# Another order of the query rows in attention: second half first, the last head from long rows to short, q and k turned one by one

## The chip, the core and the metric

The kernel runs on one core of a Trainium2 chip. The metric is the device time of one execution in microseconds (us). Five engines work side by side, each through its own queue in order: TensorE (PE in the profile, with its weight loads as PEld), VectorE (DVE), ScalarE (ACT), GpSimd (POOL) and SyncE (SP), which in this kernel issues nearly all DMA transfers. Semaphores between the queues make an instruction wait for what it needs. Matmul results go to PSUM; tiles in SBUF and PSUM come from pools with a fixed number of buffers, so that a new tile waits until the last reader of the old one in its place is done.

## The reference

One layer of a decoder on 1024 tokens of width 1024: normalise, one wide projection to q, k, v, u and g, then two branches: differential attention with 8 heads, and a convolution of width 31 per channel. Both are projected, gated and merged, and a SwiGLU follows. Attention, cut to what matters here:

```python
def probs(qb, kf):
    s = jnp.einsum('bhqd,bhkd->bhqk', qb, kf) * scale + bias
    s = jnp.where(causal, s, -jnp.inf)
    return jax.nn.softmax(s, axis=-1)

p = probs(qb1, k1f) - lamf * probs(qb2, k2f)
return jnp.einsum('bhqk,bhkd->bhqd', p, vf)
...
a = rms_norm(a, subln_w[l]) * (1.0 - lam_init)
y_a = a.reshape(B, S, ATTN_WIDTH) @ w_proj_attn[l]
```

Query block i (128 queries) sees the first (i+1) x 128 keys. Each query has two rows of scores (q1 with k1, q2 with k2).

## The kernel before

A float32 product is made from three matmuls on a high and a low part (lines 160, 161 and 162), so parts `hT_hi` and `hT_lo` of the normalised input lie in SBUF, and weights are split into `whi` and `wlo` on ScalarE and VectorE. The heads of attention are short on TensorE work, so projections that are needed later run among them as *fill*: `later` lists for each head which. An item `G` makes a slice of the gates (2 groups of 24 matmuls 128x512 each, stored in `g_d`), an item `Q` the q and k of a later head (`q_item`, 4 groups of 48 matmuls 128x256). The taps of the convolution (line 561, `acc`) fill VectorE in the same way (`bg.step`), by an estimate of each step's slack (`slack_of`).

Attention is a list of 64 steps, (head h, query block i), before in the natural order. A step does:

- `scores(h, i)`: for each of the two q/k pairs the scores in tiles of up to 512 keys (`SPLITS`), two matmuls for each (lines 1014 and 1015) into `sc`, a PSUM tile from a pool of three. VectorE adds the bias `tb`, keeps the minimum and puts the row into `E` (line 1016), ScalarE takes exp with the row sum (1021), VectorE combines both rows into `E` (1027 to 1030).
- `more(k)`: the next groups of fill. They must stand behind the scores of three steps before, and a scheduler may move them among the scores.
- `turn` of the step before: transposes of `E` (`pT`, line 1050), split by ScalarE and VectorE into `ph` and `pl`.
- `slot`: for a pair of query blocks b whose `turn` is done, `weigh` (`pW`, the product with v), two steps later `back` (`pB`, 1070), then at the head's end `subln` and `subln_T` (`pS`, 1091), which stores the head into `a_d` (SP, 1094). It also takes whatever stands in `late`.

`late` holds `turn_qk`, which transposes the q and k of half a head (`pQ`, 771), scales (778), makes the low part (780), and moves halves between partitions by DMAs on SP (781 to 792): six for q, three for k. A half is 512 queries or keys. The first half's entry is free at once, the second half's from its own head's first step. `load_bias` (tb, one buffer) goes out at a head's first step, `load_v` (vh and vl, one buffer each) after the last `weigh` of the head before.

After the 64 steps come the last `turn`, `weigh`, `back` and `subln`, and what is left of the fill: four groups, of G14 and G15. Behind that the projection of attention starts. It needs all heads: those of 0 to 3 are loaded back from `a_d` by DMAs on SP into tiles `early` (1210), split into `aTh` and `aTl` (line 120 and 125), and the first matmul of the projection reads `aTh` of head 0. The convolution's result is loaded on the same queue into `cT_lo` (1228), which takes the place of `hT_lo` in SBUF.

A scheduler sets the order of instructions on each engine from the program's order and its own estimates of time; an `after(...)` holds an instruction behind another.

Of the kernel before, what the change touches and what calls it, by code (L numbers as in the profile page):

```python
# [31 lines left out]
NT = S // P  # L32
# [25 lines left out]
def kernel(  # L58
# [28 lines left out]
    dve, act, pool, pe = nc.vector, nc.scalar, nc.gpsimd, nc.tensor  # L87
# [24 lines left out]
    def nm(s):  # L112
        uid[0] += 1
        return f"{s}_{uid[0]}"

    def f32(ap):
        return ap.bitcast(F32)

    def split_hi(dst, src):
        act.copy(dst, src)  # L120

    last_lo, last_mm = [None], [None]
# [4 lines left out]
    def after(ins):  # L127

        return nullcontext() if ins is None else tc.issue_after(ins)
# [35 lines left out]
    ident = cst.tile([P, P], F32, name="ident")  # L165
# [15 lines left out]
    one = ap.tile([1, P], F32, name="one", bufs=1)  # L181
# [58 lines left out]
    def pcol(key, k=0):  # L240
        c = col[key] + k
        return pvec[:, c : c + 1]
# [82 lines left out]
    class Stream:  # L325
# [12 lines left out]
        def next(self):  # L338
            self.fetch()
            return self.have.pop(0)  # L340
# [16 lines left out]
    def gemm_N(o, halves, shi, slo, i):  # L357
# [25 lines left out]
        ["Q1", "G0", "G1"],  # L383
        ["Q2", "G2"],
        ["Q3", "G3"],
        ["G4", "Q4", "G5"],
        ["G6", "Q5"],
        ["Q6", "G7"],
        ["G8", "G9", "Q7"],
        ["G10", "G11", "G12", "G13"],  # L390
        ["G14", "G15"],
    ]
# [344 lines left out]
    qkp = None  # L737
    T = {}
    late = []

    def q_item(h):
        halves = [ws.next(), ws.next()]
        t = {}
        T[h] = t
        for b in range(2):
            raw = qkp.tile([P, 4, 256], F32, tag="qkraw", name=nm("qkraw"), bufs=2)
            ss = sm.tile([P, 16], F32, tag="ss16", name=nm("ss16"))
            for i2 in range(2):
                o = pg()
                for e in range(2):  # L750
                    gemm_N(o[:, 256 * e : 256 * (e + 1)], halves, hT_hi, hT_lo, 4 * b + 2 * i2 + e)
                act.copy(raw[:, 2 * i2 : 2 * i2 + 2, :], o[:].rearrange("p (e c) -> p e c", c=256))
                jk = sm.tile([P, VD], F32, tag="jk", name=nm("jk"), bufs=1)[:, :HD]
                for g in range(8):
                    act.activation(  # L755
                        jk, o[:, g * HD : (g + 1) * HD], AF.Square, accum_out=ss[:, 8 * i2 + g : 8 * i2 + g + 1]
                    )
                if i2 == 0:
                    yield
            r = rstd_of(ss[:], 16, 1.0 / HD, fast=h > 0)  # L760
            r4 = raw[:].rearrange("p i (g d) -> p (i g) d", d=HD)
            dve.tensor_tensor(r4, r4, r.unsqueeze(2).to_broadcast([P, 16, HD]), op=ALU.mult)

            def turn_qk(b=b, raw=raw):


                dma = nc.sync.dma_start
                for z, key in enumerate(("q", "k")):
                    pt = pm("pQ")
                    for i in range(4):  # L770
                        pe.transpose(pt[:, i * P : (i + 1) * P], raw[:, i, z * P : (z + 1) * P], ident[:])
                    w = pcol(key + "n")

                    def part(j):
                        return qkp.tile([P, 512], F32R, tag=f"{key}s{j}", name=f"{key}s{j}_{h}_{b}", bufs=2 if key == "q" else 3)

                    s1, s2 = part(1), part(2)
                    act.activation(s1[:], pt[:], AF.Identity, scale=w)
                    lo = part(3) if key == "q" else qkp.tile([P, 512], F32R, tag="klo", name=f"klo_{h}_{b}", bufs=1)
                    dve.scalar_tensor_tensor(lo[:], pt[:], w, f32(s1[:]), op0=ALU.mult, op1=ALU.subtract)  # L780
                    dma(f32(s2[HD:, :]), f32(s1[HD:, :]))
                    if key == "q":
                        lo2 = part(4)
                        for one, two in ((s1, s2), (lo, lo2)):
                            if one is lo:
                                dma(f32(two[HD:, :]), f32(one[HD:, :]))
                            dma(f32(two[:HD, :]), f32(one[HD:, :]))
                            dma(f32(one[HD:, :]), f32(one[:HD, :]))
                        t["q", b] = (s1, lo), (s2, lo2)
                    else:  # L790
                        dma(f32(s2[:HD, :]), f32(lo[HD:, :]))
                        dma(f32(s1[HD:, :]), f32(lo[:HD, :]))
                        t["k", b] = s1, s2

            late.append((NT * h if b and h else 0, turn_qk))
            yield

    inatt = [False]
# [154 lines left out]
    n = 0  # L953
# [42 lines left out]
    def scores(h, i):  # L996
# [34 lines left out]
        dve.reciprocal(RL[h][:, i : i + 1], l[:, 0:1])  # L1031
        ES[h, i] = E[0]

    def turn(h, i):

        b = i // 2
        if (h, b) not in PT:
            ph = aps.tile([P, NT, 256], F32R, tag="ph", name=nm("ph"), bufs=1)
            pl = aps.tile([P, NT, 256], F32R, tag="pl", name=nm("pl"), bufs=1)
            pool.memset(f32(ph[:, 2 * b + 1, 0:P]), 0.0)  # L1040
            pool.memset(f32(pl[:, 2 * b + 1, 0:P]), 0.0)
            PT[h, b] = ph, pl
        ph, pl = PT[h, b]
        e = ES.pop((h, i))
        qs = slice((i % 2) * P, (i % 2 + 1) * P)
        for k0 in range(0, i + 1, 4):
            n = min(4, i + 1 - k0)
            pt = pm("pT")
            for k in range(n):
                pe.transpose(pt[:, k * P : (k + 1) * P], e[:, (k0 + k) * P : (k0 + k + 1) * P], ident[:])  # L1050
# [49 lines left out]

    inatt[0] = True
    load_v(0)
    steps = [(h, i) for h in range(H) for i in range(NT)]
    scm, weighs, backs, sublns = [], [], [], []
    fill = run(it for l_ in later for it in l_)
    plan = [sum(4 if it[0] == "Q" else 2 for it in l_) for l_ in later]
# [8 lines left out]
    last_fill = [None]  # L1115
# [6 lines left out]
    def slot(n, nq):  # L1122

        with after(last_fill[0]):
            for h, b, ar in ready(backs, n):
                back(h, b, ar)
                if b == NT // 2 - 1:
                    subln(h)
                    sublns.append((n + 1, h))
            for _ in range(nq):  # L1130
                if late[0][0] <= n:
                    late.pop(0)[1]()
            for h in ready(sublns, n):
                subln_T(h)
            for h, b in ready(weighs, n):
                backs.append((n + 2, (h, b, weigh(h, b))))
                if b == NT // 2 - 1 and h + 1 < H:
                    load_v(h + 1)

    def slack_of(h, i):  # L1140

        p = (i + 1) * plan[h] // NT - i * plan[h] // NT
        nk = (i + 1) * P
        t_pe = nk * (2.52e-3 + (2.5e-3 if i % 2 else 0.0)) + 5.15 * p
        t_dve = 0.4 + 4.2e-3 * nk + p + 0.3
        return max(0.0, t_pe - t_dve)

    slack = [slack_of(h, i) for h, i in steps]
    slack[-2:] = [0.0, 0.0]
    share = len(bg.todo) / sum(slack)  # L1150

    due = 0.0
    for n, (h, i) in enumerate(steps):
        if i == 0:
            load_bias(h)
        p = (i + 1) * plan[h] // NT - i * plan[h] // NT
# [109 lines left out]
    part = bp.tile([P, P], F32, tag="part", name="part", bufs=1)  # L1266
# [50 lines left out]
    for c in range(NE, NKT):  # L1317
        w = ws.next()
# [76 lines left out]
    for z, (c, ls) in enumerate(WO):  # L1395
# [15 lines left out]
        for t_ in ts_:  # L1411
            h = xa[t_][:, TOK[c]]
# [306 lines left out]
```

## Time and profile before

| | |
|---|---|
| median of 3 runs | 1768.08 us (1764.07 to 1768.32) |
| the profiled execution | 1767.17 us |
| its span | 1765.1 us |
| PE busy | 1749.3 us, 99% |
| DVE busy | 1272.9 us, 72% |
| ACT busy | 803.8 us, 46% |
| POOL busy | 28.8 us, 2% |
| attention with its fill | about 310 to 850 us of the span |

Span and busy times are those of the profiled execution, which is 2.07 us longer than its span. An engine's idle time counts only where it delays the end. PEclk in the page's slices is the granted clock of TensorE in tenths; where it falls to half, matmuls take twice the time.

### The profile page before, as it was taken

The page shows a single profiled execution, that of the slowest core. Times are in us where ns is not written, and L with a number is a line of the kernel's source. Part 1 is how long each engine was busy: PE and PEld are TensorE (multiplying, and loading weights), DVE is VectorE, ACT ScalarE, POOL GpSimd, SP SyncE. Part 2 cuts the span into 40 slices and gives each one's busy share as a digit, 9 for nine tenths or more (in the row PEclk, how much of TensorE's full clock was granted, in tenths as well). Part 3 has the DMA queues.
Part 4 walks back from the last instruction along what each step waited for, and adds up shares of the span by engine and source line. Part 5 has one row for each costly group of instructions (what it writes and reads, how often), then busy time and mean ns, then how long its engine had stood idle before and what let it go on. Part 6 is the DMA issues. An engine that isn't in the chain of part 4 may idle for free.

```text
span 1765.1 us, 25860 instructions
## 1 busy us (share of the span) xinstructions
PE 1749.3 (99%) x9377; PEld 1505.8 (85%) x9377; DVE 1272.9 (72%) x2173; ACT 803.8 (46%) x1885; POOL 28.8 (2%) x107
## 2 busy tenths in 40 slices
PE   9999999999999999999999999999999999999999
PEld 7898998988999998988888888888888888888887
DVE  7388878998989888986687534877667666665544
ACT  5111331657767776755557313643333333333332
POOL 2001000000000000000000000000000000000000
PEclk9999999999999999999999999999999999999999
DMA  6236363225444344352983544234544544697663
GB/s 207 95 115 215 108 181 105 89 80 159 107 123 130 88 114 135 89 166 72 327 275 108 167 167 143 90 102 147 176 149 158 177 154 138 202 360 249 214 215 131
DMA packets 255731, 274.81 MB, mean 156 GB/s; under 512 B 16066, under 2 KB 177898, under 8 KB 255604
## 3 DMA queue, kind: packets, MB, share of 16 engines
q1 hardware_dynamic: 253424, 266.40, 47.9%
q0 software_dynamic: 1744, 5.19, 1.1%
q8 instruction: 74, 1.21, 0.3%
q10 hardware_dynamic: 436, 1.58, 0.3%
q14 instruction: 53, 0.43, 0.1%
HBM read 176.07 MB, written 78.68 MB: 144 GB/s over the span
## 4 chain that ended last, share of the span: by engine, by line
PE 92%; DVE 2%; DMA 2%; ACT 2%; issue 0%; SPq 0%; ACTq 0%; DVEq 0%
PE acc L1573 22%; PE pg L160 14%; PE pg L161 14%; PE pg L162 14%; PE acc L487 12%; PE sc L1015 2%; PE sc L1014 2%; PE wo L160 2%; PE wo L162 2%; PE wo L161 2%; PE pT L1050 1%; DMA qs<-qs 1%; PE pg L840 1%; PE pW L160 1%; PE pW L162 1%; PE pW L161 1%
## 5 line engine op out<-in xcount | busy, mean ns | idle before, releaser
L561 DVE SCALAR_TENSOR_TENSOR acc<-u,cw,acc 128x1024 f32<-128x1024 f32 x240 | 306.9, 1279 | 2.7
L120 ACT CAST whi<-wraw 128x1024 fp32r<-128x1024 f32 x107 | 112.5, 1052 | 215.0 <-PE pg L161 121.7
L160 PE MATMUL pg<-hT_hi,whi 128*128 128x512 f32 x512 | 200.9, 392 | 0.8 <-ACT sgg L599 0.8
L161 PE MATMUL pg<-wlo,hT_hi 128*128 128x256 f32 x704 | 200.8, 285 | 0.0
L162 PE MATMUL pg<-hT_hi,wlo 128*128 128x512 f32 x512 | 200.8, 392 | 0.0
L161 PE MATMUL pg<-hT_lo,whi 128*128 128x512 f32 x512 | 200.6, 392 | 0.0
L160 PE MATMUL pg<-whi,hT_hi 128*128 128x256 f32 x704 | 199.9, 284 | 0.5 <-ACT jk L755 0.5
L162 PE MATMUL pg<-whi,hT_lo 128*128 128x256 f32 x704 | 200.4, 285 | 0.0
L125 DVE TENSOR_TENSOR wlo<-wraw,whi 128x1024 fp32r<-128x1024 f32 x107 | 130.5, 1219 | 67.7 <-ACT whi L120 67.4
L125 DVE TENSOR_TENSOR wlo<-draw,whi 128x1024 fp32r<-128x1024 f32 x75 | 91.8, 1224 | 89.4 <-ACT whi L120 85.6
L120 ACT CAST whi<-draw 128x1024 fp32r<-128x1024 f32 x75 | 79.1, 1055 | 129.6 <-PE acc L487 121.1
L160 PEld LDWEIGHTS pg<-whi,hT_hi 128*128 128x128 f32 x704 | 134.7, 191 | 2.3 <-ACT jk L755 0.9
L161 PEld LDWEIGHTS pg<-wlo,hT_hi 128*128 128x128 f32 x704 | 134.5, 191 | 1.3
L162 PEld LDWEIGHTS pg<-whi,hT_lo 128*128 128x128 f32 x704 | 134.7, 191 | 0.8
L487 PE MATMUL acc<-whi,wlo 128*128 128x512 f32 x308 | 119.9, 389 | 0.0
L487 PE MATMUL acc<-wlo,whi 128*128 128x512 f32 x308 | 119.8, 389 | 0.0
L160 PEld LDWEIGHTS pg<-hT_hi,whi 128*128 128x128 f32 x512 | 96.2, 188 | 20.6 <-ACT sgg L599 1.1
L1021 ACT ACTIVATE E<-E,mn 128x256 f32<-128x256 f32 (+7 forms) x128 | 99.5, 779 | 30.6 <-DVE mn L1016 28.6
L161 PEld LDWEIGHTS pg<-hT_lo,whi 128*128 128x128 f32 x512 | 96.2, 188 | 19.5 <-issue 0.6
L162 PEld LDWEIGHTS pg<-hT_hi,wlo 128*128 128x128 f32 x512 | 96.2, 188 | 19.1
L1573 PE MATMUL acc<-h_lo,whi 128*128 128x512 f32 x240 | 93.4, 389 | 0.0
L1573 PE MATMUL acc<-h_hi,whi 128*128 128x512 f32 x240 | 93.4, 389 | 0.0
(292 smaller groups left out, 4025.7 us busy)
## 6 DMA issues: line engine op xcount, KB each, us to landing
wraw<-in_w_gate_up_dram SPq DMA_DIRECT2D x44, 512.0 KB, 4.9
wraw<-in_w_in_dram SPq DMA_DIRECT2D x40, 512.0 KB, 4.4
qs<-qs SPq DMA_DIRECT2D x96, 128.0 KB, 2.3
wd<-in_w_down_dram SPq DMA_DIRECT2D x44, 256.0 KB, 3.2
tdT<-wd SPq DMA_DIRECT2D x88, 128.0 KB, 4.3
draw<-sdS SPq DMA_DIRECT2D x44, 256.0 KB, 3.9
draw<-tdT SPq DMA_DIRECT2D x44, 256.0 KB, 3.6
wraw<-in_w_in_dram SPq DMA_DIRECT2D x32, 256.0 KB, 3.6
```

Of the source, the lines that this page charges most:

```text
L120: act.copy(dst, src)
L125: last_lo[0] = dve.tensor_tensor(dst, src, f32(hi), op=ALU.subtract).ins
L160: pe.matmul(o, lh, rh, start=start, stop=False)
L161: pe.matmul(o, lh, rl, start=False, stop=False)
L162: last_mm[0] = pe.matmul(o, ll, rh, start=False, stop=stop).ins
L487: m = pe.matmul(o[s_][i][:], l_[:, ts], r_[:, 512:], start=start and j + y_ == 0, stop=j == n - 1 and y_ == 2, skip_group_check=not start,)
L561: dve.scalar_tensor_tensor(acc[0][:], us[c][:, t : t + S], cw[:, c, t : t + 1], acc[0][:], op0=ALU.mult, op1=ALU.add)
L840: last_mm[0] = pe.matmul(dst, l_, r_, start=n_ == 0, stop=n_ == len(terms) - 1).ins
L1014: pe.matmul(o[:, :w], qh[:, qs], k, start=True, stop=False)
L1015: last_mm[0] = pe.matmul(o[:, :w], ql[:, qs], k, start=False, stop=True).ins
L1021: act.activation(e[:, :nk], e[:, :nk], AF.Exp, bias=mn[:, j : j + 1], scale=-1.0, accum_out=l[:, j : j + 1])
L1573: pe.matmul(o[:], a_[x_][:, k, :], b_[y_][:, k, :], start=start and k + x_ + y_ == 0, stop=k == 3 and x_ == 1, skip_group_check=not start,)
```

## The change

- The order within a head is a table. In heads 0 to 6 the query blocks go 4, 5, 6, 7, 0, 1, 2, 3, in head 7 they go 6, 7, 4, 5, 2, 3, 0, 1. The tests for "last pair of the head" follow the table.
- `q_item` makes the second half of a head before the first, and each half gives two entries in `late`, k and q apart. At most one entry is taken in a step. An entry has a step from which it is free: for the second half's k the first step of the head before, for the first half's q the first step of its own head, else the middle of the head before.
- In three lists of `later` the item Q stands ahead of the items G.
- The number of groups in a step follows the step's number, not the query block.
- At the end one group of fill stands ahead of the last `turn` and one behind it; what is then left runs as before.

```diff
-        ["G4", "Q4", "G5"],
-        ["G6", "Q5"],
+        ["Q4", "G4", "G5"],
+        ["Q5", "G6"],
         ["Q6", "G7"],
-        ["G8", "G9", "Q7"],
+        ["Q7", "G8", "G9"],
...
-        for b in range(2):
+        for b in (1, 0):
...
-            def turn_qk(b=b, raw=raw):
+            def turn_qk(z, key, b, raw):
...
-                for z, key in enumerate(("q", "k")):
-                    pt = pm("pQ")
+                pt = pm("pQ")
...
-            late.append((NT * h if b and h else 0, turn_qk))
+            for z, key in ((1, "k"), (0, "q")):
+                free = NT * (h - 1) + (0 if key == "k" and b else NT if key == "q" and not b else NT // 2)
+                late.append((free if h else 0, lambda a_=(z, key, b, raw): turn_qk(*a_)))
...
+    ORDER = [(4, 5, 6, 7, 0, 1, 2, 3)] * (H - 1) + [(6, 7, 4, 5, 2, 3, 0, 1)]
...
-    steps = [(h, i) for h in range(H) for i in range(NT)]
+    steps = [(h, i) for h in range(H) for i in ORDER[h]]
...
-                if b == NT // 2 - 1:
+                if b == ORDER[h][-1] // 2:
...
-            for _ in range(nq):
+            for _ in range(min(nq, 1)):
...
-        if i == 0:
+        if n % NT == 0:
             load_bias(h)
-        p = (i + 1) * plan[h] // NT - i * plan[h] // NT
+        p = groups(n)
...
-    turn(*steps[-1])
-    weighs.append((n, steps[-1][:1] + (NT // 2 - 1,)))
+    for q in (turn, None):
+        with after(last_mm[0]):
+            next(fill, None)
+        last_fill[0] = last_mm[0]
+        if q:
+            q(*steps[-1])
+    weighs.append((n, steps[-1][:1] + (steps[-1][1] // 2,)))
     slot(n, len(late))
```

Lines of the kernel that stand after the new code move by a few: the scores are 1017 and 1018, the minimum 1019, the combine 1030 to 1034, `pT` 1056, `pB` 1076, the store of `a_d` 1100, `early` 1226, `cT_lo` 1244, and in `turn_qk` `pQ` 770 and the low part 779.

What the scheduler makes of it, at three places. First TensorE at the start of head 2 (counted from 0). Before, these are the scores of query block 1 (`sc_4731`, the first of them) with fill (`pg_4849`) around them:

```order
L161 MATMUL pg_4849<-wlo_4475,hT_hi 128x256
L1014 MATMUL sc_4731<-ks_2_0_4244,qs_2_0_4227 128x256
L1015 MATMUL sc_4731<-ks_2_0_4244,qs_2_0_4230 128x256
L162 MATMUL pg_4849<-whi_4474,hT_lo 128x256
L160 MATMUL pg_4849<-whi_4474,hT_hi 128x256
```

Six more fill matmuls follow there, and then transposes of the head before. Now it is query block 5, behind twelve matmuls `pW_4717`; `sc_4739` and the first matmul of `sc_4743` stand ahead of these rows, `sc_4858` to `sc_4872` are query block 6, and `E_4659` is the row of query block 4:

```order
L1018 MATMUL sc_4743<-ks_2_1_4292,qs_2_1_4370 128x256
L1017 MATMUL sc_4749<-ks_2_0_4578,qs_2_1_4368 128x512
L1018 MATMUL sc_4749<-ks_2_0_4578,qs_2_1_4373 128x512
L1017 MATMUL sc_4753<-ks_2_1_4293,qs_2_1_4368 128x256
L1018 MATMUL sc_4753<-ks_2_1_4293,qs_2_1_4373 128x256
L1017 MATMUL sc_4858<-ks_2_0_4577,qs_2_1_4367 128x512
L1018 MATMUL sc_4858<-ks_2_0_4577,qs_2_1_4370 128x512
L1017 MATMUL sc_4862<-ks_2_1_4292,qs_2_1_4367 128x384
L1018 MATMUL sc_4862<-ks_2_1_4292,qs_2_1_4370 128x384
L1017 MATMUL sc_4868<-ks_2_0_4578,qs_2_1_4368 128x512
L1018 MATMUL sc_4868<-ks_2_0_4578,qs_2_1_4373 128x512
L1056 MATMUL pT_4841<-ident,E_4659 128x128 x4
```

The scores at the head's start are wider, and no fill stands between them.

Second, VectorE at the same place. Before, with `E_4627` the row of query block 0 and `E_4730` one of block 1:

```order
L1016 ISA E_4627,mn_4625<-sc_4628,tb_4623 128x128
L1016 ISA mn_4625 128x1
L1016 ISA E_4633,mn_4625<-sc_4634,tb_4623 128x128
L1016 ISA mn_4625 128x1
L1031 RECIPROCAL rl_2_4639<-l_4626 128x1
L1016 ISA E_4730,mn_4728<-sc_4731,tb_4623 128x256
L1016 ISA mn_4728 128x1
L1027 RECIPROCAL rl_4640<-l_4626 128x1
L1028 SCALAR_TENSOR_TENSOR rl_4640<-rl_4640,neglam,l_4626 128x1
L125 TENSOR_TENSOR pl_4604<-pT_4607,ph_4603 128x4x128
L1030 SCALAR_TENSOR_TENSOR E_4627<-E_4633,rl_4640,E_4627 128x128
```

Now, from the first tile of query block 5 (`sc_4739`) to the combine of block 4 (`E_4659`):

```order
L1019 ISA E_4738,mn_4736<-sc_4739,tb_4655 128x512
L1019 ISA mn_4736 128x1
L1030 RECIPROCAL rl_4680<-l_4658 128x1
L1019 ISA E_4748,mn_4736<-sc_4749,tb_4655 128x512
L1019 ISA mn_4736 128x1
L779 SCALAR_TENSOR_TENSOR qs_2_0_4708<-pQ_4700,pvec,qs_2_0_4705 128x512
L1019 ISA E_4738,mn_4736<-sc_4743,tb_4655,mn_4736 128x256
L1019 ISA mn_4736 128x1
L1031 SCALAR_TENSOR_TENSOR rl_4680<-rl_4680,neglam,l_4658 128x1
L1019 ISA E_4748,mn_4736<-sc_4753,tb_4655,mn_4736 128x256
L1019 ISA mn_4736 128x1
L1033 SCALAR_TENSOR_TENSOR E_4659<-E_4669,rl_4680,E_4659 128x640
```

All four tiles of block 5 and the low part of the first half's q stand ahead of the combine of block 4.

Third, SP's queue at the end of attention. Before, the last two stores of head 7 (`a_d_125`), a gate's store, and at once the loads of `early`; the first `cT_lo` comes 12 transfers later:

```order
L1094 DMA a_d_125<-at_9647 128x512
L1094 DMA a_d_125<-at_9655 128x512
L600 DMA g_d_157<-sgg_9751 128x512
L1210 DMA early_0_9808<-a_d_118 128x512
L1210 DMA early_1_9812<-a_d_118 128x512
```

Now, with `cT_lo` from `c_d_134`, `135` and `136` ahead of these rows:

```order
L1244 DMA cT_lo<-c_d_137 128x512
L600 DMA g_d_157<-sgg_9779 128x512
L1100 DMA a_d_125<-at_9709 128x512
L1100 DMA a_d_125<-at_9717 128x512
L1244 DMA cT_lo<-c_d_138 128x512
L1244 DMA cT_lo<-c_d_139 128x512
L1244 DMA cT_lo<-c_d_140 128x512
L1244 DMA cT_lo<-c_d_141 128x512
L1244 DMA cT_lo<-c_d_134 128x512
L1244 DMA cT_lo<-c_d_135 128x512
L1244 DMA cT_lo<-c_d_136 128x512
L1226 DMA early_0_9808<-a_d_118 128x512
```

Eleven loads of `cT_lo` now stand ahead of the first load of `early`.

More of the change, by code (lines that the diff above doesn't have):

```diff
@@ L762, in q_item @@
             dve.tensor_tensor(r4, r4, r.unsqueeze(2).to_broadcast([P, 16, HD]), op=ALU.mult)
-            def turn_qk(b=b, raw=raw):
+            def turn_qk(z, key, b, raw):
                 dma = nc.sync.dma_start
-                for z, key in enumerate(("q", "k")):
-                    pt = pm("pQ")
[L770 to L793, printed above, removed]
@@ L795, in q_item, with part @@
-            late.append((NT * h if b and h else 0, turn_qk))
+                pt = pm("pQ")
+                for i in range(4):
+                    pe.transpose(pt[:, i * P : (i + 1) * P], raw[:, i, z * P : (z + 1) * P], ident[:])
+                w = pcol(key + "n")
+                def part(j):
+                    return qkp.tile([P, 512], F32R, tag=f"{key}s{j}", name=f"{key}s{j}_{h}_{b}", bufs=2 if key == "q" else 3)
+                s1, s2 = part(1), part(2)
+                act.activation(s1[:], pt[:], AF.Identity, scale=w)
@@ new lines, in turn_qk @@
+                lo = part(3) if key == "q" else qkp.tile([P, 512], F32R, tag="klo", name=f"klo_{h}_{b}", bufs=1)
+                dve.scalar_tensor_tensor(lo[:], pt[:], w, f32(s1[:]), op0=ALU.mult, op1=ALU.subtract)
+                dma(f32(s2[HD:, :]), f32(s1[HD:, :]))
+                if key == "q":
+                    lo2 = part(4)
+                    for one, two in ((s1, s2), (lo, lo2)):
+                        if one is lo:
+                            dma(f32(two[HD:, :]), f32(one[HD:, :]))
+                        dma(f32(two[:HD, :]), f32(one[HD:, :]))
+                        dma(f32(one[HD:, :]), f32(one[:HD, :]))
+                    t["q", b] = (s1, lo), (s2, lo2)
+                else:
+                    dma(f32(s2[:HD, :]), f32(lo[HD:, :]))
+                    dma(f32(s1[HD:, :]), f32(lo[:HD, :]))
+                    t["k", b] = s1, s2
@@ L1136, in slot, with groups, slack_of @@
                 backs.append((n + 2, (h, b, weigh(h, b))))
-                if b == NT // 2 - 1 and h + 1 < H:
+                if b == ORDER[h][-1] // 2 and h + 1 < H:
                     load_v(h + 1)
-    def slack_of(h, i):
-        p = (i + 1) * plan[h] // NT - i * plan[h] // NT
+    def groups(n):
+        h, at_ = n // NT, n % NT
+        return (at_ + 1) * plan[h] // NT - at_ * plan[h] // NT
+    def slack_of(n):
+        i, p = steps[n][1], groups(n)
         nk = (i + 1) * P
@@ L1146, in slack_of @@
         return max(0.0, t_pe - t_dve)
-    slack = [slack_of(h, i) for h, i in steps]
+    slack = [slack_of(n) for n in range(len(steps))]
     slack[-2:] = [0.0, 0.0]
@@ L1153 @@
     for n, (h, i) in enumerate(steps):
-        if i == 0:
+        if n % NT == 0:
             load_bias(h)
-        p = (i + 1) * plan[h] // NT - i * plan[h] // NT
+        p = groups(n)
         nq = len(late)
```

## The prediction

> **What bounds the kernel now.** I read the page's busy shares and slices first, then the waits of TensorE between 300 and 870 us (the eight heads and the fill around them), then the clock in windows around its two longest gaps.
>
> ```profile
> span 1765.1 us, 25860 instructions
> PE 1749.3 (99%) x9377; PEld 1505.8 (85%) x9377; DVE 1272.9 (72%) x2173; ACT 803.8 (46%) x1885; POOL 28.8 (2%) x107
> PEclk9999999999999999999999999999999999999999
> ```
>
> TensorE is busy for 99% of the span. The change adds and removes no matmul, so its work stays; only idle time and lost clock can move. What the heads have of these:
>
> ```profile
> PE sc L1014 <- DMA qs<-qs: 2.0, 1, 2.0
> PE pT L1050 <- DVE E L1030: 1.6, 1, 1.6
> PE sc L1014 <- DVE mn L1016: 0.9, 1, 0.9
> PE pg L160 <- ACT sgg L599: 0.8, 1, 0.8
> PE pW L160 <- DVE pl L125: 0.6, 1, 0.6
> PE pB L1070 <- ACT ar L1064: 0.5, 1, 0.5
> PE pg L160 <- ACT jk L755: 0.5, 2, 0.3
> PE pW L160 <- ACT jk L1079: 0.2, 1, 0.2
> PE pW L162 <- DMA vl<-v_lo: 0.2, 1, 0.2
> ```
>
> The first number is the total in us. Together they are 7.3 us. The windows around the two places of most waiting (columns: stretch, length, then busy time and instructions of PE, PEld, DVE, ACT and POOL, then the granted clock, DMA share, GB/s):
>
> ```profile
> 649.40:652.80 3.40, 1.36 (x11) 1.16 (x10) 2.62 (x10) 2.58 (x17) 0.00 (x0) 1.00 0.38 92
> 652.80:656.20 3.40, 3.40 (x16) 3.21 (x16) 1.54 (x4) 0.05 (x1) 0.19 (x1) 0.50 0.31 72
> 820.05:823.46 3.41, 1.57 (x11) 1.20 (x12) 3.05 (x5) 1.95 (x6) 0.00 (x0) 1.00 0.57 154
> 823.46:826.88 3.42, 3.42 (x17) 3.42 (x18) 0.39 (x1) 0.83 (x5) 0.00 (x0) 0.50 0.00 0
> ```
>
> Each time, a stretch of 3.4 us in which PE was busy for 1.36 or 1.57 us is followed by one of 3.4 us at half clock: 1.7 us lost, 3.4 for both. So all that the change can win in the heads is 7.3 + 3.4 = **10.7 us** of 1767.2 (the profiled execution; the span of 1765.1 and 2.1 us around it). The profiled execution lies 0.9 us under the median of the three runs, 1768.08. A measurement can tell about 0.3%, 5.3 us, from no change.
>
> **The change part by part.**
>
> *The old waits.* The longest, before the scores of row 4 in head 5:
>
> ```profile
> 643.27 0.59 ACT qs L778
> 644.38 5.89 DMA qs<-qs
> 650.33 2.17 DMA qs<-qs
> 652.53 0.59 PE sc L1014
> ```
>
> The second-half q was turned half a head before its use, and its copies stood on SP's queue behind others; the last landed 9.2 us after its scaling began. Now the q of the second half is turned up to a head earlier, and this wait goes, with its half clock. The 1.6-us wait of 820 to 823 us sits in the last head, where the longest rows came last with little work behind them; now the shortest come last. It goes with its half clock too. The remaining 3.7 us are small waits at places that all move. I take them as gone, which is generous (some will come back elsewhere; that is in the range). Next late after them are the head starts, below. Removed: **−10.7**.
>
> *q and k one by one.* The same transposes, scalings and copies, at most one of the two in a step. The k of a first half is now turned shortly before its head begins:
>
> ```profile
> L778 ACT ACTIVATE ks<-pQ,pvec 128x512 fp32r<-128x512 f32 x14 | 9.6, 685 | 3.1 <-PE pQ L771 3.1
> L780 DVE SCALAR_TENSOR_TENSOR qs<-pQ,pvec,qs 128x512 fp32r<-128x512 f32 x14 | 10.4, 745 | 1.5 <-ACT qs L778 1.4
> ks<-klo SPq DMA_DIRECT2D x32, 128.0 KB, 2.3
> ```
>
> Scaling 0.69, low part about 0.75, copies 2.3, and with two issues between them the chain takes some 6.4 us, of which two landings are the most (2 x 2.3). Counting the matmuls that stand between the transposes and the first scores gives 6.7 to 10 us of TensorE work, so the copies just fit: 0, and up to 0.5 us at one or two heads if an earlier copy holds SP. They are issued behind no load that waits. The bias load stands ahead of a head's first scores as before.
>
> *The head starts.* This is the first new cost. A row of i+1 key tiles (i from 0) needs 2 score tiles up to 512 keys and 4 above, from a pool of three. A head used to begin with one-tile rows that have fill matmuls among them. It now begins with rows 4, 5, 6. In heads 1, 2, 4 and 5 (counted from 0) the order puts no fill between the scores of rows 5 and 6 and the transposes of row 4. So TensorE has eight score matmuls of row 5 and six of row 6 to do while VectorE must take row 5 out of PSUM, the second-half combine of row 4, and in between a q low part:
>
> ```profile
> L1016 DVE CUSTOM_DVE_ANT_0 E<-sc,tb 128x512 f32<-128x512 f32 x80 | 54.5, 685 | 8.8 <-PE sc L1015 5.2 <-PE pT L1050 3.0
> L1016 DVE DVE_READ_ACCUMULATOR2_ANT mn<- 128x1 f32 x192 | 15.9, 83 | 0.0
> L1016 DVE CUSTOM_DVE_ANT_0 E<-sc,tb,mn 128x256 f32<-128x256 f32 x16 | 7.6, 474 | 1.0 <-PE sc L1015 1.0
> L1027 DVE RECIPROCAL rl<-l 128x1 f32<-128x1 f32 x64 | 10.1, 158 | 16.0 <-ACT E L1021 15.7
> L1028 DVE SCALAR_TENSOR_TENSOR rl<-rl,neglam,l 128x1 f32<-128x1 f32 x64 | 13.8, 215 | 0.9
> L1030 DVE SCALAR_TENSOR_TENSOR E<-E,rl,E 128x640 f32<-128x640 f32 x8 | 7.0, 879 | 0.0
> ```
>
> and for TensorE's pace a row of the chain, 1602 matmuls of 128x512 in a row:
>
> ```profile
> 1169.66 364.57 PE acc L1573 x1602
> ```
>
> VectorE, in the order of its queue: first tile 0.685 + 0.083 = 0.77, reciprocal 0.16, second tile 0.77, q's low part 0.75, third and fourth 0.474 + 0.083 = 0.56 each, the small scale 0.22 between them, combine 0.88: 4.65 us. It starts when TensorE has made the first tile, two matmuls of 128x512. The row of the chain gives 364.57 / 1602 = 0.228 us for one of these, 0.46 for two; 5.1 us in all. TensorE's burst: 4 x 0.228 and 4 at half that width (0.114, an estimate by columns) for row 5, 4 x 0.228 and 2 x 0.171 for row 6: 2.6 us. The difference, **2.5 us**, TensorE waits, whether for a score tile or for the combine. The other three heads are put together alike, with 2.9, 2.8 and 2.2 by the same count; I take 4 x 2.5 = **+10.0**. Below it is bounded by 0 (VectorE ahead, a gap like the one that follows) and by this row of the kernel before, where scores stood close and a tile was not free:
>
> ```profile
> 392.77 0.44 PE L1014 MATMUL sc<-ks,qs 128*128 128x384 f32 x1 [0.94 <-DVE mn L1016]
> ```
>
> 0.94 us each would make 3.8; above, 2.9 x 4 = 11.6. I take the count, since the queue of VectorE stands written out and the row's case had less on it. Heads 3, 6 and 7 keep fill among these scores: 0.
>
> *The clock.* Gaps of 0.94 us did not halve it; 2.04 of 3.40 us idle did. A stall of 2.5 us lies between, and its place in the 3.4-us stretches decides; it is split in parts besides. I give one of the four a halved stretch: **+1.7** (0 to 6.8).
> The Trainium skill's page "TensorE: Matmul & The Clock Gate", section "HAM oscillation — how this bites in real kernels", asks for gaps of more than about 3.4 us before the clock drops. The rows above speak against it here (2.04 us in a stretch 40% busy was enough). By that rule no head start would lose clock, and the sum would be 1.7 lower, 1779.5.
>
> *The end of attention.* The second new cost. One of the two last groups of fill (G15's end) used to run after the last weighing; now one is ahead of the last `turn` and one behind it, and no fill is left behind the last weighing and the last transposes. On SP's queue before (start, length):
>
> ```profile
> 846.96 3.75 SPq L1210 DMA_DIRECT2D early<-a_d  x8
> 855.61 4.28 SPq L1228 DMA_DIRECT2D cT_lo<-c_d  x7
> 860.26 0.32 SPq L1293 DMA_DIRECT2D gt<-g_d  x1
> ```
>
> and on the chain of waits at the same place:
>
> ```profile
> 842.50 0.87 PE pS L1091 x8
> 846.96 3.31 DMA early<-a_d
> 850.37 0.63 ACT aTh L120
> ```
>
> The loads of the finished heads (`early`) were issued at 846.96, landed 3.31 us later, were split in 0.63, and the projection began at once behind the last fill. In the new order eleven `cT_lo` loads, a `g_d` store and two `a_d` stores stand on SP ahead of the first `early`. The first `cT_lo` takes the place of `hT_lo`, so it waits for the last matmul of the last fill group, and all fourteen wait with it; and behind that matmul TensorE has nothing but 1.0 us of `pS` until the projection, whose first matmul needs the first `early`. From that matmul's end: seven `cT_lo` issues took 860.26 − 855.61 = 4.65 us, 0.66 each. Eleven to fourteen of them are 7.3 to 9.3 us; landing 3.31, split 0.63, handovers 0.1, less the 1.0 of `pS` (0.87 in the row): 10.3 to 12.3 idle. I take **+11.3**. An idle time of this length fills whole stretches, so the stretch behind it runs at half clock: **+1.7** (to 3.4 if it straddles two).
>
> *Sum.* 1767.2 − 10.7 + 0 + 10.0 + 1.7 + 11.3 + 1.7 = **1781.2 us**.
>
> **The rivals.**
>
> *Not slower (0.14): the head starts cost nothing.* The place is VectorE's queue in front of rows 5 and 6. If TensorE arrives late at row 5 because of `pB`, `pQ` and twelve `pW` matmuls before it, VectorE will have finished more, and the four tiles overlap. For it: VectorE is 72% busy, has slack at such places, and a tap or two may fall elsewhere. Against it: what it must do stands behind the first score tile of row 5 and cannot begin sooner. It decides once VectorE's chain there is under 3 us. Then the time is 1767.2 − 10.7 + 10.3 to 11.3 + 1.7 = 1768.5 to 1769.5, within 0.3% of before.
>
> *Worse (0.18): the head starts are not four stalls of 2.5 but lose the clock each time, and the taps of the convolution push VectorE further back.* Those are 1.276 us each by line 561's rows, and one that lands ahead of the chain adds itself. Four half stretches are 6.8 in place of 1.7, at the upper stall of 11.6, with 3.7 us of the old waits still there and a tail of 12.3 + 3.4:
>
> ```profile
> L561 DVE SCALAR_TENSOR_TENSOR acc<-u,cw,acc 128x1024 f32<-128x1024 f32 x124 | 158.3, 1276 | 0.1
> ```
>
> 1767.2 − 7.0 + 11.6 + 6.8 + 15.7 = 1794; about 1790 to 1796.
>
> *Faster (0.03): the tail does not wait, because the loads ahead of `early` are ready in time.* That asks for the place of `hT_lo` to come free before the last fill ends, and the last fill group itself reads it. With head starts of 0 as well it would be 1767.2 − 10.7 = 1756.5.
>
> *The turn doesn't come early.* If the limit of one per step left a q or k behind, the 2.0-us wait would stay with its half clock, 3.7 us more, at most at one head; inside the range.
>
> **How the numbers follow.** Forecast 0.65, not slower 0.14, worse 0.18, faster 0.03. The range is **1768 to 1792**: it takes in the whole of "not slower" and the lower half of "worse", and leaves out 0.12 (the upper half of "worse" and "faster") and the few that unknown sizes add. Of the forecast's own part (1774 to 1788) nearly nothing is under 1773.4 (0.3% over the median). So: faster 0.04, the same 0.13, slower 0.83.
>
> **What would show it.** In the profile after: the wait of `sc` on `qs` gone; among TensorE's waits a group of about 10 us for `aTh` or `early` near 850 us, and behind it a stretch at 0.50; at the start of heads 1, 2, 4 and 5 waits of 2 to 3 us of `sc` on `mn` or of `pT` on `E`, and none such in heads 3, 6 and 7. I'd be wrong if the idle time before the first projection matmul were under 5 us, or the four starts cost under 4 us together, or if the half-clock stretches were over four.

## The result, and the profile after

The changed kernel takes **1786.4 us** (median of 4 runs, 1785.1 to 1788.3), the kernel before 1767.9. The ratio is 1.011, interval 1.0093 to 1.0128. The forecast was 1781.2 in a range of 1768 to 1792, so sign and range held and the loss was 4 to 5 us larger than forecast. The page of the changed kernel's profiled execution (1785.5 us):

```profile
span 1783.4 us, 25851 instructions
PE 1751.6 (98%) x9377; PEld 1504.5 (84%) x9377; DVE 1272.5 (71%) x2173; ACT 801.3 (45%) x1885; POOL 28.9 (2%) x107
```

TensorE's busy time rose by 2.3 us, the span by 18.3. The waits of TensorE in the heads and at their end, from 300 to 890 us (total, times, longest):

```profile
PE pg L160 <- ACT aTh L120: 13.9, 1, 13.9
PE sc L1017 <- DVE mn L1019: 4.2, 8, 1.0
PE sc L1017 <- DMA ks<-klo: 3.3, 3, 2.2
PE pT L1056 <- DVE E L1033: 0.6, 2, 0.4
PE pT L1056 <- ACT jk L755: 0.4, 1, 0.4
PE pT L1056 <- DVE rl L1034: 0.2, 1, 0.2
```

The wait of `sc` on `qs` is gone, and so is the 1.6-us wait of `pT` on `E`. In their place stand the wait for `aTh` at the projection, eight waits for a score tile, and a wait that was not forecast, for `ks`. Where the clock was halved, in windows (columns as before):

```profile
577.10:580.52 3.42, 1.23 (x8) 0.98 (x8) 1.93 (x3) 0.07 (x1) 0.00 (x0) 1.00 0.17 41
580.52:583.93 3.41, 3.41 (x16) 3.21 (x15) 2.60 (x6) 0.00 (x0) 0.00 (x0) 0.50 0.02 5
...
857.00:860.40 3.40, 0.00 (x0) 0.00 (x0) 0.00 (x0) 0.00 (x0) 0.00 (x0) 0.50 1.02 375
...
867.20:870.65 3.45, 3.43 (x8) 2.75 (x9) 3.45 (x6) 3.16 (x6) 0.00 (x0) 0.50 1.03 388
```

One half-clock stretch follows the wait for `ks`. Four in a row follow the start of the stall at the end, from 857.0 to 870.65 us; three of these lie on an idle TensorE and one on work behind the stall. A sum over the whole trace: for each matmul, the time to the next one's start less the median for its shape. This lost time holds idle time, slow first matmuls behind a gap and lost clock, and its difference is that of the spans.

| lost time, us | before | after |
|---|---|---|
| start, to 300 us | 8.1 | 8.0 |
| heads, 300 to 845 us | 15.0 | 17.5 |
| end of attention, 845 to 900 us | 1.5 | 17.3 |
| the rest | 2.0 | 2.1 |
| all | 26.7 | 45.0 |

So the end of attention cost 15.8 us and the heads, all gains and losses together, 2.5. The end on SP's queue, and the first split that TensorE waits for on ScalarE:

```profile
852.27 1.74 SPq L1244 DMA_DIRECT2D cT_lo<-c_d  x4
854.40 0.32 SPq L600 DMA_DIRECT2D g_d<-sgg  x1
854.83 0.86 SPq L1100 DMA_DIRECT2D a_d<-at  x2
855.75 4.72 SPq L1244 DMA_DIRECT2D cT_lo<-c_d  x7
860.79 5.32 SPq L1226 DMA_DIRECT2D early<-a_d  x8
```

```profile
866.55 3.90 ACT L120 CAST aTh<-early 128x512 fp32r<-128x512 f32 x6 [11.49 <-DMA early<-a_d]
```

The first `cT_lo` goes out as the last fill matmul ends, at 852.27; the first `early` 8.5 us later; its split begins 5.8 us after that.

The late k, on the chain of waits ahead of head 4's first scores:

```profile
570.66 0.76 DVE klo L779
571.42 0.48 SPq L996
...
572.55 4.82 DMA ks<-ks
...
577.39 2.46 DMA ks<-klo
...
579.99 0.47 PE sc L1017
```

L996 is the bias load of 512 KB. The copy of k issued behind it took 4.8 us to land. The issues of such first copies (size, median from issue to landing), in the kernel before, in the changed kernel and in e5 below, where the bias load goes out behind them:

```profile
ks<-ks SPq DMA_DIRECT2D x16, 128.0 KB, 2.3
```

```profile
ks<-ks SPq DMA_DIRECT2D x16, 128.0 KB, 3.2
```

```profile
ks<-ks SPq DMA_DIRECT2D x16, 128.0 KB, 2.2
```

### The profile page after: what moved, and what is told of

Its sections match the earlier page's. It is cut to its first block, busy times and chain, and to the rows that moved or that the text cites. A ratio compares the mean times of both kernels' runs of the same rounds, so it can differ in the third digit from the quotient of the medians.

```text
span 1783.4 us, 25851 instructions
## 1 busy us (share of the span) xinstructions
PE 1751.6 (98%) x9377; PEld 1504.5 (84%) x9377; DVE 1272.5 (71%) x2173; ACT 801.3 (45%) x1885; POOL 28.9 (2%) x107
## 4 chain that ended last, share of the span: by engine, by line
PE 92%; DMA 3%; DVE 2%; ACT 2%; issue 1%; SPq 0%; DVEq 0%; ACTq 0%
PE acc L1589 21%; PE pg L160 14%; PE pg L161 14%; PE pg L162 14%; PE acc L487 12%; PE sc L1017 2%; PE sc L1018 2%; PE wo L162 2%; PE wo L161 2%; PE wo L160 2%; PE pT L1056 2%; PE pW L160 1%; PE pW L161 1%; PE pW L162 1%; PE pg L843 1%; PE pQ L770 1%
## 5 line engine op out<-in xcount | busy, mean ns | idle before, releaser
L1024 ACT ACTIVATE E<-E,mn 128x640 f32<-128x640 f32 (+7 forms) x128 | 99.8, 780 | 34.5 <-DVE mn L1019 32.3
```

Source lines behind the costliest of these rows:

```text
L1024: act.activation(e[:, :nk], e[:, :nk], AF.Exp, bias=mn[:, j : j + 1], scale=-1.0, accum_out=l[:, j : j + 1])
```

## The experiments

Each ratio is to the kernel before, measured beside the run in question. A difference between two changed kernels is one of medians that were not all measured together; the kernel before took 1765.9 to 1767.9 us beside them, so such a difference is uncertain by about 2 us.

| run | us | ratio to before, interval | lost in heads, at the end |
|---|---|---|---|
| changed kernel | 1786.4 | 1.0110, 1.0093 to 1.0128 | 17.5, 17.3 |
| e1 | 1780.9 | 1.0077, 1.0062 to 1.0092 | 16.6, 11.2 |
| e2 | 1776.5 | 1.0058, 1.0043 to 1.0073 | 25.0, 0.8 |
| e3 | 1783.3 | 1.0092, 1.0077 to 1.0107 | 14.8, 18.0 |
| e4 | 1784.7 | 1.0099, 1.0083 to 1.0116 | 18.4, 17.8 |
| e5 | 1781.6 | 1.0085, 1.0070 to 1.0100 | 13.6, 17.9 |
| e6 | 1788.1 | 1.0120, 1.0104 to 1.0135 | 18.5, 18.0 |
| e7 | 1774.6 | 1.0045, 1.0029 to 1.0062 | 20.6, 2.4 |
| e8 | 1772.6 | 1.0033, 1.0020 to 1.0046 | 20.8, 3.4 |
| e9 | 1767.9 | 1.0013, 1.0004 to 1.0022 | 15.1, 3.3 |
| e10 | 1769.5 | 1.0023, 1.0014 to 1.0033 | 14.4, 4.9 |
| e11 | 1779.7 | 1.0083, 1.0069 to 1.0097 | 25.8, 4.9 |
| e12 | 1776.9 | 1.0065, 1.0052 to 1.0077 | 21.6, 4.8 |

The two lost times are those of the table above, from each run's own trace. In the runs with e8's end a wait of 1.7 us for `ar` falls on both sides of the border at 845 us: among the heads in e8, e9 and e10, at the end in e11 and e12.

### The end of attention: e1, e2, e8

e1, `early` ahead of `cT_lo`:

```diff
+            if h < 4:
+                last_early = ld.ins
...
-            nc.sync.dma_start(cc[c], c_d[c][:, cs])
+            with after(last_early):
+                nc.sync.dma_start(cc[c], c_d[c][:, cs])
```

> The changed kernel with the cT_lo loads queued on SP behind the last of the eight early loads. In the trace TensorE stands idle for 13.9 us before the projection. Theory (the order on SP's queue makes most of it): the early loads then wait only for the two a_d stores, whose tiles are ready about 2.5 us after the last fill matmul; with 0.9 for the two stores, 3.3 for the landing and 0.6 for the split the idle time becomes about 6.4 us, so 7.5 us less, and about 1779 us, with the half-clock stretch behind it still there. Rival (with no fill left behind the last weighing the loads are late in any order, because their place comes free late or the link is full): 12 to 14 us idle, 1785 to 1787.

The wait fell from 13.9 to 8.9 us, the time by 5.5. The order on SP was a good third of the stall, less than expected: the landing took 5.3 us where 3.3 was expected, though no `cT_lo` stood ahead (critical chain):

```profile
855.32 5.33 DMA early<-a_d
```

A weight load and the two stores of `a_d` stood just ahead of it; which transfer made it slow is not shown. The rest is the chain from `pS` over the two stores to the landing, with nothing on TensorE beside it.

e2, the end as before:

```diff
-    for q in (turn, None):
-        with after(last_mm[0]):
-            next(fill, None)
-        last_fill[0] = last_mm[0]
-        if q:
-            q(*steps[-1])
+    turn(*steps[-1])
```

> The changed kernel with its end undone alone: no fill group ahead of or behind the last turn, all four groups of G14 and G15 behind the last weighing as before; all orders of the heads as changed. Theory (the two groups moved forward open the end): the idle time before the projection falls from 13.9 to under 1 us and the half-clock stretch of 1.7 us goes, so about 15 us less, near 1771. Rival (the last head's new order, from long rows to short, is what makes SP's queue late): a stall of 5 us or more stays, 1777 or above.

The stall before the projection went as the theory said: 0.8 us are lost there. But the time fell by 10 us and not by 15, since the last head now lacked the fill. Its short rows came to wait, and the windows there show three half-clock stretches in a row:

```profile
PE pW L160 <- ACT ph L120: 1.7, 2, 0.9
PE pW L161 <- DVE pl L125: 1.1, 1, 1.1
...
827.00:830.40 3.40, 1.39 (x8) 1.19 (x9) 3.40 (x5) 2.58 (x11) 0.00 (x0) 0.94 0.58 154
830.40:833.82 3.42, 2.86 (x11) 1.68 (x10) 2.27 (x6) 1.51 (x7) 0.61 (x3) 0.50 0.34 143
833.82:837.20 3.38, 2.71 (x9) 2.35 (x10) 0.42 (x1) 0.99 (x5) 0.00 (x0) 0.50 0.03 11
837.20:840.65 3.45, 3.45 (x11) 2.70 (x10) 0.00 (x0) 0.00 (x0) 0.00 (x0) 0.56 0.00 0
```

So the four last groups have two places that want them, the last rows' chain and the way from the last weighing to the loads. The changed kernel leaves the second bare, e2 the first.

e8, `early` first, and of the two groups behind the last weighing one behind the last `pB` and one behind the last `pS`:

```diff
+    for m in (last_pB[0], last_pS[0]):
+        with after(m):
+            next(fill, None)
```

> The changed kernel with its end put in another order: cT_lo loads behind the early loads as in e1_early_first, and of the two fill groups behind the last weighing one is held behind the last pB and one behind the last pS, so that 5.5 us of fill lie behind the stores of the last head. Theory (what is left of the stall in e1, 8.9 us, is the chain from pS over the two a_d stores to the landing of early, with no work over it): 5.5 us of it are covered and about 3.5 us stay; if that is short enough for only one half-clock stretch, 1775 to 1777. Rival (the early loads come late whatever lies over them, since SP first waits for the last gate's store): 8 us or more idle, 1780 or above.

```profile
PE pg L160 <- ACT aTh L120: 1.8, 2, 1.4
PE pB L1077 <- ACT ar L1071: 1.7, 1, 1.7
PE sc L1018 <- DMA ks<-klo: 3.8, 3, 2.3
```

1772.6 us, 13.8 less than the changed kernel and 8.3 less than e1, whose order of the loads it has as well. The stall is 1.4 us (0.4 more a little later), the price is a wait of 1.7 for the last `ar`, and no clock is lost at the end. That settles the end: the same amount of work, put over the chain that the loads hang on and with the loads ahead of `cT_lo`, takes the stall away.

### The late k: e3, e5, e7

e3, up to two turns in a step: `range(min(nq, 2))` for `range(min(nq, 1))`.

> The changed kernel with up to two q or k turned in one step instead of one. Theory (k of the first half comes one step too late behind q of the second half): the three waits for ks, 3.3 us together, and the half-clock stretch behind the longest of them (1.7 us) go, so about 5 us less, near 1781. Rival (the copies are slow because the bias load of 512 KB and two weight loads share the queues with them, not because they start late): the waits stay within 1 us of 3.3, 1785 to 1787.

```profile
PE pg L160 <- ACT jk L755: 1.6, 1, 1.6
PE sc L1017 <- DMA ks<-klo: 1.1, 1, 1.1
```

The waits for `ks` went from 3.3 to 1.1 us and the half-clock stretch went. 3 us were won and not 5: a wait of 1.6 for ScalarE's `jk` came instead. The run does not tell the theory from its rival, though: with the new order of turns the bias load at head 4 stood on SP behind the copies of k (575.30 us against 572.49 for the first copy), and that copy had landed when the next went out at 574.75, 2.3 us later.

e5, the bias load behind the copies of k:

```diff
-        nc.sync.dma_start(tb[:], skew.rearrange("(p l) -> p l", l=TL - 1)[:, :S])
+        with after(last_k[0]):
+            nc.sync.dma_start(tb[:], skew.rearrange("(p l) -> p l", l=TL - 1)[:, :S])
```

> The changed kernel with the bias load of a head (512 KB) queued on SP behind the three copies of the first half's k. In the trace the first of these copies at head 4 took 4.8 us to land, against a median of 2.3, with the bias load issued just ahead of it. Theory A (the bias load makes the copy slow): the wait of 2.2 us at head 4 falls to nothing, its half-clock stretch goes, and the three waits for ks fall from 3.3 to under 1 us: near 1782. Theory B (the k turns begin too late by more than that, and the loads of weights ahead cost as much): the waits fall by less than 1 us, and the bias, now later, may add a wait of VectorE at the head's start: 1785 to 1788.

```profile
PE sc L1019 <- DMA ks<-klo: 1.1, 1, 1.1
DVE E L1021 <- DMA tb<-t_d: 3.4, 2, 2.3
```

Theory A: 4.9 us less, no half-clock stretch in the heads, waits for `ks` 1.1 us. At head 4 the wait fell from 2.2 to 1.1 us and not to nothing: the first copy went out 0.9 us earlier (571.61 for 572.55) and the next could follow 3.8 us later, with a load of weights now just ahead of it. Over all heads the median landing of the first copies fell from 3.2 to 2.2 us. So the bias load was the larger part of what made the copies late, and a load of weights in its place costs as well. Its own new place has a price that Theory B named: VectorE waited 3.4 us for the bias, where it had no such wait in the changed kernel. TensorE's waits for score tiles did not grow by it (3.2 us, from 4.2).

e7, the kernel before with k and q split and one per step, in its own order of rows:

> The kernel before with only this part of the change: k and q are two entries, k first, at most one taken in a step; all orders, the lists of the fill and the end as before. Theory (the split by itself moves the copies by a step and costs or wins little; the cost comes only where a k must be ready at a head's start): 1765 to 1771, with the wait of 2 us for qs at head 5 about as before. Rival (one entry per step is itself too slow and makes q or k late): 3 us or more of new waits of sc on qs or ks and half-clock stretches, 1772 or above.

The theory falls: 1774.6 against 1766.8, 7.9 us slower. The time is the rival's, but its half-clock stretches did not come: no clock was halved in the heads. The five largest waits of TensorE:

```profile
PE pg L160 <- ACT jk L755: 2.6, 3, 1.3
PE pW L160 <- DVE t L616: 1.8, 1, 1.8
PE pW L162 <- DMA vl<-v_lo: 1.4, 2, 1.1
PE pW L160 <- DMA vh<-v_hi: 1.3, 1, 1.3
PE sc L1017 <- DMA qs<-qs: 1.2, 1, 1.2
```

They are not at one place: by their names, v loads and q copies that meet on SP, and work of ScalarE and VectorE that comes late. What makes it late is not shown. In the old order the split alone has a price that the prediction set at nothing. In the new order the same limit, loosened to two, was worth 3 us (e3), and nothing once the bias load stood right (e10).

### The last head, and the head starts: e6, e4, e11, e12

e6, `ORDER = [(4, 5, 6, 7, 0, 1, 2, 3)] * H`.

> The changed kernel with head 7 in the same order as the others (4, 5, 6, 7, 0, 1, 2, 3) instead of from its longest rows to its shortest. Theory (what the last head's order wins is small, since with one fill group on each side of the last turn the chain of its last rows is covered either way): within 3 us of the changed kernel, 1784 to 1789, with the stall of 13 to 14 us before the projection unchanged. Rival (short rows at the very end are what keeps TensorE busy there): 2 us or more of new waits between 815 and 850 us and a half-clock stretch, 1790 or above.

1788.1: the last head's special order is worth 1.7 us between the medians, 2.8 when each is taken against the kernel before beside it, which is hardly more than the noise. The stall before the projection stays, and no new wait stands in the last head.

```profile
PE pg L160 <- ACT aTh L120: 14.6, 1, 14.6
PE sc L1017 <- issue: 2.7, 1, 2.7
PE pg L160 <- ACT jk L755: 2.6, 2, 2.3
```

The edit is in head 7 alone, and yet heads 4 and 5 changed: the wait for k at head 4 is gone, and waits of 2.7 us (at 641 us, until the last copy of k had landed) and 2.3 us (at 673 us) came. So a difference of 2 or 3 us between two of these kernels can come from another place than the edit.

e4, `NT + 1` for `NT` as the step from which a first-half q is free:

> The changed kernel with the first-half q of a head turned one step later, so that its low part (0.75 us on VectorE) no longer stands between the score tiles of row 5 and the combine of row 4 at a head's start. Theory (VectorE's chain there is what TensorE waits for): each of the four head starts loses up to 0.75 us of about 2.0, 2 to 3 us in all, near 1784. Rival (TensorE waits for the three score buffers through the exp and the minimum, not through the length of this chain): the starts keep their 8 us, 1786 to 1787.

```profile
PE sc L1017 <- issue: 2.6, 1, 2.6
PE sc L1017 <- DVE mn L1019: 1.6, 5, 0.5
```

The time is in the expected place, but the gain did not come through. The waits for score tiles fell from 4.2 to 1.6 us, as the theory of VectorE's chain asks. Head 5's start then waited 2.6 us, until the last copy of its k had landed, and two half-clock stretches followed: the lost time in the heads rose by 0.8.

e9 is e8 and e5 together, e10 adds e3, e11 adds to e10 a fill group forced between rows 5 and 6, e12 adds e4 to e9. The added part of e11:

```diff
+        early_fill = h and n % NT == 2
+        if early_fill:
+            with after(scm[-1]):
+                next(fill, None)
+            last_fill[0] = last_mm[0]
+        with after(last_fill[0] if early_fill else None):
+            scores(h, i)
```

> e8_ps_first and e5_tb_behind_k together: the end with fill behind the last pS, and the bias load behind the k copies. Theory (the two places are apart and their prices add): 1772.6 less the 4.9 us that the bias load's place won by itself, near 1768, level with the kernel before. Rival (they are not independent, since the scheduler moves fill between them): 1771 or above.

The prices add: 1767.9, and no half-clock stretch ahead of the kernel's end.

> e9_ps_tb with up to two q or k turned in a step. Theory (k is then a step earlier and nothing of its waits is left, 1.1 us in e5): 1 us less than e9, near 1767. Rival (the turns crowd a step and delay other work, as the 1.6-us wait for jk in e3 showed): no gain or up to 2 us more than e9.

1769.5, nothing won over e9. In its trace the heads lost 0.7 us less than in e9, near what the theory says, with a wait of 1.6 us for `jk` among them, as the rival says. The end lost 1.6 more: the waits for `aTh` are the same as in e9 (1.4 and 0.4 us), but in e10 a half-clock stretch followed. So the run doesn't decide between the two.

> e10_ps_tb_two with a whole fill group of 5.5 us forced between the scores of rows 5 and 6 at every head's start but the first. Theory (TensorE waits at the head starts because scores of rows 5 and 6 stand with no fill between them and VectorE cannot keep up): the waits of sc on mn and of pT on E at heads 1, 2, 4 and 5 fall from about 8 us of lost time in the changed kernel to under 2, about 6 us less than e10. Rival (the fill is taken from in front of the head's first scores, where it covers the copies of k): new waits of sc on ks of 2 us and more, with half-clock stretches, eat the gain, no better than e10.

```profile
PE sc L1020 <- DVE mn L1022: 6.7, 7, 2.1
PE sc L1020 <- issue: 3.1, 1, 3.1
```

10 us slower than e10. The theory had the place wrong: with the fill moved behind row 5, rows 4 and 5 stand close instead, and the waits for a score tile grew from 2.5 (e10) to 6.7 us, the longest, 2.1 us at head 1, ahead of the last tile of row 4. The rival came true at head 5: the wait of 3.1 us ended 2.3 us after the last copy of its k was issued, and two half-clock stretches followed.

> e9_ps_tb with the first-half q turned a step later as in e4_q_later. Theory (VectorE's chain at a head's start is 0.75 us shorter, and with the bias load behind k the late k that spoilt e4 is gone): 2 to 3 us less than e9, near 1766. Rival (the later turn again moves the order so that a k comes late): a wait of sc on ks or of no named releaser over 2 us and a half-clock stretch, 1769 or above.

```profile
PE sc L1020 <- DVE mn L1022: 5.1, 7, 1.9
PE sc L1020 <- issue: 2.6, 1, 2.6
```

1776.9, the rival: again a late k at head 5, although the bias load was out of its way, and waits for score tiles of 5.1 us. Its copies were not slow (2.2 us); they went out late.

None of these beats the kernel before. The nearest, e9, is 0.13% slower (0.04 to 0.22).

## Why the prediction was right, by its own steps

| step | forecast, us | measured, us |
|---|---|---|
| old waits and their clock | −10.7 | −10.6 |
| four head starts | +10.0 | +8.1 |
| clock after a head start | +1.7 | 0 |
| k turned shortly before its head | 0 | +3.3, and 1.7 of clock |
| the end of attention | +13.0 | +15.8 |
| sum | +14.0 | +18.3 |

- **Old waits.** The 2.0-us wait for `qs` and the 1.6 of the last head went, each with its half-clock stretch: 7.0 us, shown by the trace. Of the rest of the heads' lost time, 8.0 us before and 4.4 now are left when the items of this table are taken out: 3.6 less, against the 3.7 that were called generous. This is a remainder, and which small waits make it up is not shown.
- **Head starts.** They came at heads 1, 2, 4 and 5 and not at 3, 6 and 7, as the written-out queues said: 2.3, 1.6, 2.5 and 1.7 us lost, where 2.2 to 2.9 were counted; the waits named there are 5.4 us together, and the rest does not show as idle time. The size was taken a fifth too high. At head 4 the trace shows why: VectorE took row 5's first tile at 587.70 us and was done with the combine at 592.2, a chain of 4.5 us for the 4.65 counted, but until 588.82 TensorE still had twelve `pW` matmuls to do. That its chain is the cause is supported by the names of the waits and by e4, where they fell with the q taken out of it. It isn't settled: e4, e11 and e12 each brought another wait, and no run isolates the chain.
- **Clock.** One half-clock stretch was forecast for the heads and one came, but by another cause: it followed the wait for `ks`. No head start had over 1.4 us of idle time in a stretch of 3.4. Four of the five half-clock stretches are those at the end. The prediction named more than four as a sign that it was wrong, and by this count it was; but only two of the five fell on work.
- **k turned late.** This is the step that failed. Its cover was right: at head 4 TensorE had 7.9 us of work behind the transposes. The chain was not: it took 9.9 us from the scaling to the last landing and not 6.4. The first copy took 4.8 us, not 2.3, behind a load of 512 KB on the same queue. "The bias load stands ahead of a head's first scores as before" was noted and its weight not drawn: as before it stood there, but what stood behind it was new. e5 shows this as the larger part of the cause. The step made the largest error, 5.0 us with its clock. The clock's 1.7 is partly chance: in e2 the wait at head 4 was 2.1 us, and no clock was halved there.
- **The end.** The mechanism was right: fourteen transfers ahead of the first `early`, all behind the last fill matmul, and 8.5 us until it was issued (7.3 to 9.3 forecast). One reading was not: fill is left behind the last weighing. The trace has 48 matmuls of it there, two groups, but all ahead of `pS`; before, 33 of 96 stood behind `pS`, over the stores and loads. The term mis-sized is the landing, taken at 3.3 us from the first of eight loads in the kernel before, whose median was 4.7: it took 5.8 to the start of the split, with eleven `cT_lo` loads ahead and the DMA share at 1.02 in the window above. That these eleven made it slow is not shown, as e1 has 5.3 without them.
- **The rivals.** "Not slower" asked for VectorE's chain under 3 us; it took 4.5 at head 4, and the head starts cost 8. "Worse" forecast a half stretch at each head start; none came. The result lies nearer to its 1790 than to the forecast, by the late k and the end and not by its mechanism.
- **Luck.** That the total came within 5 us is partly luck: the errors of +5.0 (k) and +2.8 (the end) were made smaller by −1.9 (head starts) and −1.7 (clock).

## What to carry to other kernels

When work is moved onto a queue, price its transfers by what stands ahead of them at that place, not by a landing time read elsewhere: the late k (5.0 us with its clock) and most of the 2.8 us missing at the end were such landing times. When filler work is moved earlier, ask what it covered: the same groups were wanted at the last rows and over the final stores and loads, and one group placed behind the last transposes, with the order of e1, took a 14-us stall down to 1.4 (e8). Each attempt to ease the head starts by order alone (e4, e11, e12) brought a late k at head 5, of 2.6 to 3.1 us.

## What the runs showed of the hardware

The half clock keeps to a grid. In all traces of this study the half-clock stretches lasted 3.4 us or whole multiples of it (but for the one that the end of the kernel cuts off), and began on the same grid of 3.413 us, counted from the first change of the clock. What decides, as far as these traces tell, is TensorE's idle time within one stretch of the grid, not the length of a gap. Every full-clock stretch with 1.79 us or more of idle time was followed by half clock, 18 in all; of 44 stretches with 0.96 to 1.74 us of it one was (1.60 us, e6), so the border is not sharp. Two nearest each other, from e7 and then e10 (windows, 1.69 and 1.61 us busy of 3.40):

```profile
404.90:408.30 3.40, 1.69 (x14) 1.72 (x15) 3.11 (x13) 2.92 (x20) 0.00 (x0) 1.00 1.14 263
408.30:411.70 3.40, 3.04 (x26) 2.84 (x26) 2.85 (x3) 0.96 (x4) 0.37 (x2) 1.00 0.35 93
```

```profile
850.00:853.40 3.40, 1.61 (x6) 0.74 (x5) 1.89 (x3) 2.97 (x5) 0.00 (x0) 1.00 0.86 268
853.40:856.80 3.40, 3.40 (x9) 2.64 (x9) 3.40 (x6) 3.26 (x7) 0.00 (x0) 0.50 1.03 389
```

So a gap that straddles a border of the grid can cost no clock where a shorter one inside a stretch costs 1.7 us: the wait of 2.1 us at head 4 of e2 lay across a border and halved nothing, while in the e10 window above the longest gap was 1.4 us.

The Trainium skill's page "TensorE: Matmul & The Clock Gate" gives this window, 3413 ns and free-running, in its section "What's actually happening"; the trace agrees with its length (3.413 us). Its section "HAM oscillation — how this bites in real kernels", which the prediction weighed, sets the limit at gaps of about 3.4 us; there the trace differs, with 2.19 us of idle time at head 4 enough.
